# Low-key product of the banded and differential logits: 64 or 128 rows

## Chip, cores and metric

The kernel runs on one core of a Trainium2 chip. The metric is the device time of one execution in microseconds (us), as the median of several runs. The engines go by the profile's names: PE is TensorE's matmuls and PEld its weight loads, DVE is VectorE, ACT is ScalarE, POOL is GpSimd, SP is SyncE, which issues the loads of weights.

## What is computed

The program is a bidirectional encoder of two layers over 512 tokens with 1024 features, in float32. In each layer come a feed-forward block, three attentions whose gated outputs are added, a second feed-forward block and an embedding gate. The change touches two of the attentions. Cut to their logits (the first is banded, a token sees those at most 128 away):

```python
# windowed grouped-query attention: 16 heads of 64 columns, 4 heads of keys
logits = jnp.einsum('bqkgd,bskd->bkgqs', qj, kj).astype(jnp.float32) * scale + bias
logits = jnp.where(valid, logits, NEG_INF)
...
# differential attention: 8 heads, two maps (c) of 64 columns in each
logits = jnp.einsum('bqhcd,bkhcd->bchqk', qj, k).astype(f32) * scale + bias
probs = jax.nn.softmax(logits, axis=-1)
attn = probs[:, 0] - lam * probs[:, 1]
```

Both contract over 64 columns. The scale is 1/8.

## The kernel before

**Split operands.** PE takes operands in a reduced format (float32r). A float32 operand is therefore split into two parts, hi (a rounded copy, made on ACT) and lo (the rest, a subtraction on DVE), whose sum is the operand. A product then takes three matmuls: hi by hi, lo by hi, hi by lo. All of them go through one helper, `mm`, so that nearly every matmul has line L165 in the profile; they are told apart by the names of their tiles.

**Two parts in one product.** A head of 64 columns fills only half of the 128 rows of the array. `q_pair` (L541) uses this: for a pair of heads it makes two tiles of queries, of which tile 0 has hi on rows 0 to 63 and lo on rows 64 to 127, and tile 1 the other way round. The keys' hi part lies on both halves. So one matmul of 128 rows computes q_hi k_hi + q_lo k_hi. The second product, q_hi k_lo, takes only the half of the rows on which q_hi lies (`own`): 64 rows. Both add into one bank of PSUM.

**Who makes the low keys.** `swa_k` (L554) makes the windowed keys, 2 heads at a time, and writes k_lo on both halves, with two subtractions for each head. `diff_k` (L590) makes the differential keys of a pair of maps: four copies on ACT (hi of each map on both halves) and two subtractions on DVE (L599), one for each map, each on the map's own half of one tile `kl`.

**Stages.** The names in the profile give layer, kind and head: m0C3s is the bank of logits (s) of differential head 3 in layer 0; A are heads of the latent attention (16), C differential ones (8), B windowed ones (16); p is a head's tile of probabilities, t its transposes (pth and ptl their hi and lo parts), o its output. Each layer's attention runs A, then C, then B. A differential head has 4 blocks of 128 queries and two maps, so 8 logit tiles of 128 x 512. A windowed head has 4 blocks, each with the two or three blocks of keys around it: 128 x 256 at the two ends and 128 x 384 in the middle.

A logit tile goes from PE to DVE (bias added and the row's minimum, L805 or L747), to ACT (exponential and sum, L807 or L749), to POOL and DVE (division by the sum), back to PE (transposes, L635), to ACT and DVE (their hi and lo parts, L638 and L639), and to PE for the values.

**What sets the order.** Other work of PE (projections of queries, keys, values, gates, and the output product) is cut into pieces that a queue, `Filler`, hands out between the steps of the heads; each piece has a due head, and the queue runs at the lowest even pace that meets these. A pair of differential queries and its keys are due one head ahead of their own. After that a scheduler orders each engine's instructions by their dependences. PSUM has five banks for the heads' steps and three for the filling work. Weights come as 456 chunks of 512 KB by SP, split into hi on ACT (L75) and lo on DVE or, in the attention, on POOL (L76). Tiles of 128 x 512 come from 79 slots.

Of the kernel before, what the change touches and what calls it, by code (L numbers as in the profile page):

```python
# [23 lines left out]
T = 512  # L24
TB = T // P
# [11 lines left out]
# columns of the table of small per-partition values, for each layer  # L37
# [8 lines left out]
class Weights:  # L46
    """All weights as one stream of [128, 1024] chunks, in the order of their use: loaded ahead, then split
    into two float32r parts whose sum is the float32 weight."""
# [41 lines left out]
class Filler:  # L90
    """Pieces of tensor-engine work in a queue, run between the steps of the attention: at the least even pace at
    which each piece ends before the step that it is due at."""
# [44 lines left out]
def encoder_kernel(ctx: ExitStack, tc: tile.TileContext, ins, out):  # L137
# [18 lines left out]
    def PS(name, kind=None):  # L156
        """A bank of PSUM: of those of the attention's steps (s), of those of the work between them (a), or of both
        by turns."""
        if kind is None:
            kind = CYCLE[turn[0] % len(CYCLE)]  # L160
            turn[0] += 1
        return psp.tile([P, 512], F32, tag="ps" + kind, name=name, bufs=BANKS[kind])
# [9 lines left out]
    def split(src, name):  # L172
        """src as two float32r tiles."""
        hi, lo = S(name + "h", F32R), S(name + "l", F32R)
        nc.scalar.copy(hi, src)
        nc.vector.tensor_sub(lo, src, hi.bitcast(F32))
        return hi, lo

# [32 lines left out]
    def constants():  # L211
        nc.gpsimd.dma_start(perm, ins["perm"])
        for l in range(L):
            s = slice(l * NH, (l + 1) * NH)
            nc.vector.tensor_scalar(neg_sink[:, s], small[:, l * S_N + S_SINK:l * S_N + S_SINK + NH], -1.0, None, op0=ALU.mult)
            nc.vector.tensor_scalar(sub_gain[:, l:l + 1], col(l, S_SUB), 1.0 - lambda_init(l), None, op0=ALU.mult)
            lv = S(f"lamv{l}")
            nc.gpsimd.dma_start(lv[:, 0:256], ins["lam"][l])
            e = tiny(f"lam{l}")
            for j in range(2):  # L220
                pr = S(f"lamp{l}{j}")
                nc.vector.tensor_mul(pr[:, 0:64], lv[:, j * 128:j * 128 + 64], lv[:, j * 128 + 64:j * 128 + 128])
                nc.vector.tensor_reduce(e[:, j:j + 1], pr[:, 0:64], axis=AX.X, op=ALU.add)
            nc.scalar.activation(e[:, 2:4], e[:, 0:2], AF.Exp)
            # -(exp(a) - exp(b) + init)
            nc.vector.tensor_scalar(e[:, 4:5], e[:, 3:4], -lambda_init(l), None, op0=ALU.add)
            nc.vector.tensor_sub(neg_lam[:, l:l + 1], e[:, 4:5], e[:, 2:3])
# [10 lines left out]
    def bias_vectors():  # L238
        """The bias of each head over the distance, negated; in the window's, 1e30 outside it."""
        for i in range(3):  # L240
            ps = PS(f"bv{i}")
            heads = slice(0, NH) if i == 0 else slice(NH, NH + NHD)
            n = heads.stop - heads.start
            nc.tensor.matmul(ps[0:n, :], tab[0][0:33, heads], oh[i][0:33, :], start=True, stop=True)
            bv = S(f"bvs{i}")
            nc.vector.tensor_copy(bv[0:n, :], ps[0:n, :])  # L246
            if i == 0:
                nc.gpsimd.dma_start(bias_s, bv[0:n, :])  # L248
            else:
                nc.gpsimd.dma_start(bias_d[:, (i - 1) * 512:i * 512], bv[0:n, :])  # L250
        for vec, copies in ((bias_s, copies_s), (bias_d, copies_d)):
            for i in range(vec.shape[0]):
                nc.gpsimd.dma_start(copies[i], vec[i:i + 1, :].to_broadcast([P, vec.shape[1]]))

    def strip(vec, row, cols, tag, bufs, name):
        """[128, cols]: the head's vector at 127 - p + c, from the copies of it that lie one after the other."""
        t = sb.tile([P, cols], F32, tag=tag, name=name, bufs=bufs)
        n = vec.shape[2]
        at = vec[row, 0:1, 127:128]
        nc.gpsimd.dma_start(t, bass.AP(tensor=at.tensor, offset=at.offset, ap=[[n - 1, P], [1, cols]]))  # L260
        return t

# [1 line left out]
    def root_table():  # L264
        """Loads the square root's table ahead of its use."""
        tc.keep_in_program_order(nc.scalar.activation(tiny("root")[:, 0:1], eps, AF.Sqrt))
# [7 lines left out]
    class Norm:  # L274
        """Root mean square over the features (partitions and tiles), for all tokens."""
# [13 lines left out]
        def add_last(self, src, c):  # L289
            """The columns c of the last tile."""  # L290
            sq = S(f"{self.name}sq{self.i}{c.start}")
            nc.scalar.activation(sq[:, c], src[:, c], AF.Square)
            self.engine.tensor_tensor(self.acc[:, c], self.acc[:, c], sq[:, c], op=ALU.add)
# [18 lines left out]
    class Prep:  # L312
        """The tiles of h as they end: gained and split; the norm's factor comes in after the product."""
# [18 lines left out]
    def proj(ps, w, z, i0=0, n=KT, cols=P):  # L332
        """ps += (128 columns of weights)^T z over n k tiles; yields the work done."""
        wh, wl = w
        for k in range(n):
            c = slice(i0 + k * cols, i0 + k * cols + cols)
            mm3(ps, wh[:, c], wl[:, c], z[k][0], z[k][1], k == 0, k == n - 1)
            if side:
                side.popleft()()
            yield 3  # L340

    def together(pss, ws, z):
        """Several such products, a k tile of each at a time."""
        gens = [proj(ps, w, z, cols=ps.shape[0]) for ps, w in zip(pss, ws)]
        for _ in range(KT):
            for g in gens:
                next(g)
# [59 lines left out]
    def mix(l, prep, p2):  # L407
# [3 lines left out]
        # per-layer input: 0.5 * p W, kept in DRAM until the layer's end  # L411
# [34 lines left out]
        # latents  # L446
# [32 lines left out]
        # keys of a pair of heads, three pairs by turns: rows 0-63 | 64-127 are (own, rope) or (rope, own)  # L479
# [23 lines left out]
        # pieces of work for the tensor engine  # L503
        merged = [None] * KT

        def mla_v(g):
            wh, wl = W.get(("mla_v", l, g))
            vs = [S(f"{name}va{g}_{tb}", F32R) for tb in range(TB)]
            for tb in range(TB):
# [7 lines left out]
                # a pair of heads: hi lo | lo hi  # L517
# [25 lines left out]
        def q_pair(key, at, j):  # L543
            """Two 64-wide queries, times -1/8: (hi, lo) and (lo, hi) on the two halves of the rows."""
# [22 lines left out]
        def swa_v():  # L567
            ws = W.get(("vb", l, 0), ("vb", l, 1))
            for tb in range(TB):
# [10 lines left out]
                for j in range(2):  # L580
                    # a head: hi lo hi
# [8 lines left out]
        def diff_k(j):  # L590
# [3 lines left out]
            kl = S(f"{name}kc{j}l", F32R)  # L594
            for e in range(2):
                own = halves[e]
                for r in halves:
                    nc.scalar.copy(ks[e][r], ps[own])  # L598
                nc.vector.tensor_sub(kl[own], ps[own], ks[e][own].bitcast(F32))  # L599
# [25 lines left out]
        class Head:  # L625
# [22 lines left out]
            def out64(self, i, lhs, gated):  # L648
                """Values of 64 columns as (hi, lo) or (lo, hi): the two halves of the rows are added. Both heads of
                a pair end on the rows that they have in the merged output."""  # L650
# [64 lines left out]
        class Swa(Head):  # L715
# [16 lines left out]
            def logits(self):  # L732
# [3 lines left out]
                own = halves[i % 2]  # L736
                m, sums = tiny(f"{self.name}m"), tiny(f"{self.name}s")
                self.p = []
                for q in range(TB):
# [5 lines left out]
                    mm(ps, qs[own, c], kl[own, k0:k1], False, True)  # L745
# [34 lines left out]
        class Diff(Head):  # L780
# [10 lines left out]
            def logits(self):  # L791
# [4 lines left out]
                for q in range(TB):  # L796
                    c = slice(q * P, (q + 1) * P)
                    bs = self.strip[:, (TB - 1 - q) * P:(TB - 1 - q) * P + T]
                    for e in range(2):
                        own, x = halves[e], e * TB + q  # L800
                        ps = PS(f"{self.name}s{q}{e}", "s")
                        mm(ps, qs[e][:, c], ks[e], True, False)
                        mm(ps, qs[e][own, c], kl[own], False, True)
# [47 lines left out]
        # the heads' steps, and what has to be there before them  # L851
# [12 lines left out]
        for due, key, units, gen in sorted(work, key=lambda x: x[0]):  # L864
            # a pair's keys overwrite those of three pairs before
# [10 lines left out]
        for n, hd in enumerate(heads + [None]):  # L876
# [6 lines left out]
            def run_steps(upto):  # L883
                """What is left of the head before, once so many quarters of this one's logits are under way."""
                while steps and STEP_AT[steps[0][0]] <= upto:
                    steps.pop(0)[1]()
# [31 lines left out]
    def w_out(l):  # L918
        """Four output tiles at a time, over the merged tiles in their order; two of these in each piece."""
# [27 lines left out]
    def ple(l, prep, after, last=None):  # L947
# [6 lines left out]
        for d in range(KT):  # L954
# [8 lines left out]
            if d == KT - 1 and last is not None:  # L963
                # the columns in two halves, for a short way to the end
# [24 lines left out]
    for l in range(L):  # L989
# [24 lines left out]
        def last(d, c):  # L1014
            if c.stop == T:
                # the table of the square root is loaded by the time of the norm
# [25 lines left out]
# latent norms: k tiles of other products between their squares and their sums  # L1042
LEAD = 16
# logit tiles after which the finished ones are normalised
NORMALISE = {"Mla": 2, "Swa": 4, "Diff": 4}
# the shares of a head's filling work that go between its logits and after its transposes
# [5 lines left out]
def _chunk(ins, key):  # L1052
    """A weight chunk of the stream: [128, up to 1024], rows of the weight on the partitions."""
# [85 lines left out]
def build(nc, L):  # L1139
    """The program; the arrays' shapes; the order of the weight chunks."""  # L1140
# [39 lines left out]
```

## Time and profile before

| | before |
|---|---|
| median of 3 runs | 3098.61 us (3098.36 to 3099.18) |
| span of the profiled execution | 3096.5 us, 2.1 us under that median |
| granted clock of TensorE, mean | 0.998 |
| PE, PEld, DVE busy | 3056.6, 2463.9, 1812.5 us |
| ACT, POOL busy | 1423.1, 748.1 us |
| layer 0: A heads / C heads / B heads | 444 to 712 / 712 to 924 / 924 to 1110 us |
| layer 1: C heads / B heads | 2245 to 2456 / 2456 to 2643 us |

The page is of one execution; the trace has no time of its own for that execution besides the span, which runs from the first instruction to the last. The bounds of the stages are read from the starts of the heads' first logits and, at the end, of the last head's values; neighbouring stages overlap by some microseconds, since the steps of one head end in the next one.

### The profile page before, as it was taken

The numbers are of one execution on the slowest core, as the hardware profiler recorded it, in microseconds if no ns is written. First come the engines' busy times: TensorE is split into PE (matmuls) and PEld (weight loads), VectorE is DVE, ScalarE is ACT, GpSimd is POOL, SyncE is SP. The second block draws the span as 40 slices with busy tenths as digits, with TensorE's granted clock in tenths as the row PEclk, the third lists the DMA queues.
The fourth block names the chain that finished last, engine by engine and source line by source line (L and its number), as shares of the span: only waits on it lengthen the run. The fifth ranks groups of instructions, "written<-read, shape, count | busy, mean of one in ns | idle before, by whom it ended". The sixth has DMA issues, their size and how long they took to land.

```text
span 3096.5 us, 37450 instructions
## 1 busy us (share of the span) xinstructions
PE 3056.6 (99%) x14206; PEld 2463.9 (80%) x14206; DVE 1812.5 (59%) x2812; ACT 1423.1 (46%) x2511; POOL 748.1 (24%) x709
## 2 busy tenths in 40 slices
PE   8999999999999999999999999999999999999997
PEld 7888878887777788888888887788877777888886
DVE  6444586535686665444664445765467766654446
ACT  4322356645666653223432223565556666422234
POOL 0010014444445440000200001244444445200003
PEclk9999999999999999999999999999999999999999
DMA  4263431112122233333333334211222122333332
GB/s 151 97 222 99 136 109 59 58 62 80 61 74 80 66 105 96 97 101 95 123 102 96 96 96 152 89 55 55 75 73 72 61 66 66 116 95 96 99 99 89
DMA packets 81524, 287.74 MB, mean 93 GB/s; under 512 B 10382, under 2 KB 12430, under 8 KB 81344
## 3 DMA queue, kind: packets, MB, share of 16 engines
q1 hardware_dynamic: 66960, 240.42, 24.7%
q0 software_dynamic: 12080, 42.00, 3.9%
q10 hardware_dynamic: 2304, 2.94, 0.3%
q8 instruction: 111, 1.82, 0.2%
q14 instruction: 69, 0.57, 0.1%
HBM read 274.76 MB, written 18.94 MB: 95 GB/s over the span
## 4 chain that ended last, share of the span: by engine, by line
PE 95%; DVE 2%; ACT 2%; issue 1%; POOL 0%; DMA 0%; ACTq 0%; DVEq 0%; POOLq 0%
PE ffn10g L165 4%; PE ffn10u L165 4%; PE ffn21g L165 4%; PE ffn20g L165 4%; PE ffn21u L165 4%; PE ffn20u L165 4%; PE ffn21d L165 4%; PE ffn11d L165 4%; PE ffn20d L165 4%; PE ffn10d L165 4%; PE ffn11u L165 4%; PE ffn11g L165 4%; PE wo L165 3%; PE ple L165 3%; PE m1qc L165 2%; PE m0qc L165 2%
## 5 line engine op out<-in xcount | busy, mean ns | idle before, releaser
L75 ACT CAST whi<-wraw 128x1024 fp32r<-128x1024 f32 x456 | 478.2, 1051 | 1093.8 <-issue 379.7
L76 DVE TENSOR_TENSOR wlo<-wraw,whi 128x1024 fp32r<-128x1024 f32 x312 | 383.6, 1232 | 124.2 <-ACT whi L75 123.8
L76 POOL TENSOR_TENSOR wlo<-wraw,whi 128x1024 fp32r<-128x1024 f32 x144 | 351.2, 2441 | 411.2 <-ACT whi L75 375.9
L287 POOL TENSOR_TENSOR pg1sq<-pg1sq,pg1sq 128x512 f32<-128x512 f32 x7 | 11.1, 1586 | 345.0 <-ACT pg1sq L282 345.0
L287 POOL TENSOR_TENSOR pg0sq<-pg0sq,pg0sq 128x512 f32<-128x512 f32 x7 | 11.1, 1586 | 345.0 <-ACT pg0sq L282 345.0
L419 POOL DMA_DIRECT2D h_dram<-wo0h x8 | 4.3, 541 | 341.2 <-DVE wo0h L371 341.2
L371 DVE SCALAR_TENSOR_TENSOR x<-ffn10d,x 128x512 f32<-128x512 f32 x48 | 32.9, 690 | 40.9 <-PE ffn10d L165 40.9
L371 DVE SCALAR_TENSOR_TENSOR wo0h<-ffn11d,wo0h 128x512 f32<-128x512 f32 x48 | 32.9, 690 | 40.9 <-PE ffn11d L165 40.9
L371 DVE SCALAR_TENSOR_TENSOR wo1h<-ffn21d,wo1h 128x512 f32<-128x512 f32 x48 | 32.9, 690 | 38.7 <-PE ffn21d L165 38.7
L371 DVE SCALAR_TENSOR_TENSOR wo0h<-ffn20d,wo0h 128x512 f32<-128x512 f32 x48 | 32.9, 690 | 38.1 <-PE ffn20d L165 38.0
L388 DVE TENSOR_TENSOR ffn20u<-ffn20u,f_0r 128x512 f32<-128x512 f32 x22 | 15.2, 691 | 62.0 <-PE ffn20u L165 62.0
L388 DVE TENSOR_TENSOR ffn21u<-ffn21u,f_1r 128x512 f32<-128x512 f32 x22 | 15.2, 691 | 62.0 <-PE ffn21u L165 62.0
L419 POOL DMA_DIRECT2D h_dram<-x x8 | 4.3, 540 | 190.3 <-DVE x L371 190.3
L388 DVE TENSOR_TENSOR ffn10u<-ffn10u,f_0r 128x512 f32<-128x512 f32 x22 | 15.2, 691 | 59.8 <-PE ffn10u L165 59.8
L388 DVE TENSOR_TENSOR ffn11u<-ffn11u,f_1r 128x512 f32<-128x512 f32 x22 | 15.2, 691 | 59.5 <-PE ffn11u L165 59.5
L386 DVE TENSOR_TENSOR ffn20g<-ffn20g,f_0r 128x512 f32<-128x512 f32 x22 | 15.2, 692 | 47.0 <-PE ffn20g L165 46.9
L386 DVE TENSOR_TENSOR ffn21g<-ffn21g,f_1r 128x512 f32<-128x512 f32 x22 | 15.2, 692 | 46.6 <-PE ffn21g L165 46.6
L386 DVE TENSOR_TENSOR ffn10g<-ffn10g,f_0r 128x512 f32<-128x512 f32 x22 | 15.2, 691 | 44.4 <-PE ffn10g L165 44.4
L386 DVE TENSOR_TENSOR ffn11g<-ffn11g,f_1r 128x512 f32<-128x512 f32 x22 | 15.2, 690 | 44.5 <-PE ffn11g L165 44.5
L287 POOL TENSOR_TENSOR f_1sq<-f_1sq,f_1sq 128x512 f32<-128x512 f32 x14 | 21.0, 1501 | 58.5 <-ACT f_1sq L282 58.3
L248 POOL DMA_DIRECT2D bias_s<-bvs x1 | 0.5, 519 | 142.5 <-DVE bvs L246 142.5
L598 ACT CAST m0kc<-m0kc 64x512 fp32r<-64x512 f32 x32 | 18.5, 580 | 17.2 <-PE m0kc L165 7.9
(5072 smaller groups left out, 10401.3 us busy)
## 6 DMA issues: line engine op xcount, KB each, us to landing
wraw<-in_wall SPq DMA_DIRECT2D x456, 512.0 KB, 3.5
copies_s<-bias_s POOLq DMA_DIRECT2D x16, 256.0 KB, 7.5
copies_d<-bias_d POOLq DMA_DIRECT2D x8, 512.0 KB, 12.8
h_dram<-x POOLq DMA_DIRECT2D x8, 256.0 KB, 2.9
pp_dram<-m0ppt POOLq DMA_DIRECT2D x8, 256.0 KB, 5.6
wo0h<-h_dram POOLq DMA_DIRECT2D x8, 256.0 KB, 4.8
ple0p<-pp_dram POOLq DMA_DIRECT2D x8, 256.0 KB, 4.6
h_dram<-wo0h POOLq DMA_DIRECT2D x8, 256.0 KB, 2.7
```

The source lines that it names most:

```text
L75: self.nc.scalar.copy(hi, raw)
L76: self.lo_engine.tensor_tensor(lo, raw, hi.bitcast(F32), op=ALU.subtract)
L165: nc.tensor.matmul(ps, lhsT, rhs, start=start, stop=stop, skip_group_check=True)
L248: nc.gpsimd.dma_start(bias_s, bv[0:n, :])
L287: self.engine.tensor_tensor(self.acc, self.acc, sq, op=ALU.add)
L371: nc.vector.scalar_tensor_tensor(h[d], ps, 0.5, h[d], op0=ALU.mult, op1=ALU.add)
L386: nc.vector.tensor_mul(g1, pg, rb)
L388: nc.vector.tensor_mul(u1, pu, rb)
L419: nc.gpsimd.dma_start(h_dram[d], h[d])
L598: nc.scalar.copy(ks[e][r], ps[own])
```

## The change

The second product now takes all 128 rows, with k_lo on both halves: it computes q_hi k_lo + q_lo k_lo, so the small product of the two low parts comes in as well. The windowed keys are as before. `diff_k` now makes two tiles of low keys for each pair, one for each map, with the map's k_lo on both halves. This takes four subtractions for each pair where there were two, and one slot more. The rest of the diff takes out comments.

```diff
             ks = [S(f"{name}kc{j}{e}", F32R) for e in range(2)]
-            kl = S(f"{name}kc{j}l", F32R)
+            kl = [S(f"{name}kc{j}l{e}", F32R) for e in range(2)]
             for e in range(2):
                 own = halves[e]
                 for r in halves:
                     nc.scalar.copy(ks[e][r], ps[own])
-                nc.vector.tensor_sub(kl[own], ps[own], ks[e][own].bitcast(F32))
+                for r in halves:
+                    nc.vector.tensor_sub(kl[e][r], ps[own], ks[e][own].bitcast(F32))
             got["kc", j] = (ks, kl)
...
                 ks, kl = got["kb", i // 4]
-                own = halves[i % 2]
...
                     mm(ps, qs[:, c], ks[:, k0:k1], True, False)
-                    mm(ps, qs[own, c], kl[own, k0:k1], False, True)
+                    mm(ps, qs[:, c], kl[:, k0:k1], False, True)
...
                     for e in range(2):
-                        own, x = halves[e], e * TB + q
+                        x = e * TB + q
                         ps = PS(f"{self.name}s{q}{e}", "s")
                         mm(ps, qs[e][:, c], ks[e], True, False)
-                        mm(ps, qs[e][own, c], kl[own], False, True)
+                        mm(ps, qs[e][:, c], kl[e], False, True)
```

The instructions of PE stay the same in number, those of DVE change at `diff_k`, and the scheduler then places some rows otherwise. SP and POOL keep their order, and so do PE and DVE in the windowed heads. On DVE, at the first pair of differential keys of layer 0, behind the reductions of latent head A11 and ahead of the transposes' lo parts of head A10, there stood:

```order
L691 TENSOR_REDUCE m0A11m_4851<-m0A11s3_4896 128x1
L697 RECIPROCAL m0A11s_4852<-m0A11s_4852 128x2
L599 TENSOR_TENSOR m0kc0l_4908<-m0kc0_4825,m0kc00_4906 64x512
L599 TENSOR_TENSOR m0kc0l_4908<-m0kc0_4825,m0kc01_4907 64x512
L639 TENSOR_TENSOR m0A10ptl0_4934<-m0A10t0_4928,m0A10pth0_4933 128x512
L639 TENSOR_TENSOR m0A10ptl1_4943<-m0A10t1_4937,m0A10pth1_4942 128x512
```

In the changed program the same place on DVE reads (lines from there on are one higher; m0kc0l0 and m0kc0l1 are the two tiles of low keys):

```order
L692 TENSOR_REDUCE m0A11m_4851<-m0A11s3_4896 128x1
L698 RECIPROCAL m0A11s_4852<-m0A11s_4852 128x2
L600 TENSOR_TENSOR m0kc0l0_4908<-m0kc0_4825,m0kc00_4906 64x512 x2
L600 TENSOR_TENSOR m0kc0l1_4909<-m0kc0_4825,m0kc01_4907 64x512 x2
L640 TENSOR_TENSOR m0A10ptl0_4937<-m0A10t0_4931,m0A10pth0_4936 128x512
L640 TENSOR_TENSOR m0A10ptl1_4946<-m0A10t1_4940,m0A10pth1_4945 128x512
```

Each row of low keys has become two, at the same place between the same neighbours. On PE, in the logits of differential head C1, whose tiles alternate with the filling product m0gc (a gate), there stood:

```order
L165 MATMUL m0C1s11_6153<-m0kc1l_5282,m0qc11_5225 128x512
L165 MATMUL m0gc4_6107<-m0u4h_2767,whi112_5973 128x512
L165 MATMUL m0gc4_6107<-m0u4h_2767,wlo112_5974 128x512
L165 MATMUL m0gc4_6107<-m0u4l_2768,whi112_5973 128x512
L165 MATMUL m0C1s20_6168<-m0kc10_5280,m0qc10_5224 128x512
L165 MATMUL m0C1s20_6168<-m0kc1l_5282,m0qc10_5224 128x512
L165 MATMUL m0gc4_6107<-m0u5h_2774,whi112_5973 128x512
L165 MATMUL m0gc4_6107<-m0u5h_2774,wlo112_5974 128x512
L165 MATMUL m0gc4_6107<-m0u5l_2775,whi112_5973 128x512
L165 MATMUL m0C1s21_6177<-m0kc11_5281,m0qc11_5225 128x512
```

And the same stretch of PE in the changed program:

```order
L165 MATMUL m0C1s11_6168<-m0kc1l1_5286,m0qc11_5228 128x512
L165 MATMUL m0gc4_6122<-m0u4h_2767,whi112_5985 128x512
L165 MATMUL m0gc4_6122<-m0u4h_2767,wlo112_5986 128x512
L165 MATMUL m0gc4_6122<-m0u4l_2768,whi112_5985 128x512
L165 MATMUL m0gc4_6122<-m0u5h_2774,whi112_5985 128x512
L165 MATMUL m0gc4_6122<-m0u5h_2774,wlo112_5986 128x512
L165 MATMUL m0gc4_6122<-m0u5l_2775,whi112_5985 128x512
L165 MATMUL m0C1s20_6183<-m0kc10_5283,m0qc10_5227 128x512
L165 MATMUL m0C1s20_6183<-m0kc1l0_5285,m0qc10_5227 128x512
L165 MATMUL m0gc4_6122<-m0u6h_2781,whi112_5985 128x512
```

The logit tile m0C1s20 has gone behind the next three rows of the gate. The order gives the output's shape alone, so the second product reads the same in both; how many rows of the array it takes doesn't show here.

## The prediction

> **What bounds the kernel now.** I read the page first: which engine is busy, and whose work makes up the chain that ended last.
>
> ```profile
> PE 3056.6 (99%) x14206; PEld 2463.9 (80%) x14206; DVE 1812.5 (59%) x2812; ACT 1423.1 (46%) x2511; POOL 748.1 (24%) x709
> PE 95%; DVE 2%; ACT 2%; issue 1%; POOL 0%; DMA 0%; ACTq 0%; DVEq 0%; POOLq 0%
> ```
>
> TensorE (PE) is busy for 3056.6 of 3096.5 us and carries 95% of the chain. So time comes off the kernel where PE's own instructions get shorter. The average says little about the two stages that the change touches, so I read next the busy time in stretches: the differential heads and the windowed heads, of layer 0 and then of layer 1 (columns: stretch, its length, then PE, weight loads, VectorE (DVE), ScalarE (ACT), GpSimd (POOL)).
>
> ```profile
> core 0: us, PE busy (x) PEld busy (x) DVE busy (x) ACT busy (x) POOL busy (x), PEclk, DMA share, GB/s
> 712.00:924.00 212.00, 210.80 (x1003) 155.57 (x1002) 151.95 (x279) 134.51 (x260) 92.95 (x73) 1.00 0.23 71
> 924.00:1110.00 186.00, 184.59 (x883) 140.07 (x882) 119.70 (x293) 123.06 (x302) 92.51 (x103) 1.00 0.22 68
> 2245.00:2456.00 211.00, 209.79 (x998) 154.72 (x997) 153.50 (x278) 133.72 (x258) 91.49 (x71) 1.00 0.21 67
> 2456.00:2643.00 187.00, 185.60 (x887) 140.59 (x886) 120.18 (x295) 122.81 (x302) 92.81 (x103) 1.00 0.21 67
> ```
>
> PE is busy all through there at a granted clock of 1.00, and no other engine passes 73%. The list of waits for PE over both stages of layer 0 is short:
>
> ```profile
> PE m0C4o L165 <- DVE m0C4ptl L639: 1.2, 1, 1.2
> PE m0B5o L165 <- DVE m0B5ptl L639: 0.7, 1, 0.7
> PE m0B6o L165 <- DVE m0B6ptl L639: 0.5, 1, 0.5
> ```
>
> PE waits for others 2.4 us of 398. But a busy PE isn't PE at its peak, since the ends of matmuls are modelled: the start of one to the start of the next tells what each really takes. So the last view is PE's order of time, around two logit tiles. First a differential head (columns: start in us, duration, then line, operation, tiles, rows*columns of the stationary operand, moving operand):
>
> ```profile
> 711.76 0.39 PE L165 MATMUL m0gc<-m0u1l,whi 128*128 128x512 f32 x1
> 711.99 0.39 PE L165 MATMUL m0gc<-m0u2h,whi 128*128 128x512 f32 x1
> 712.21 0.39 PE L165 MATMUL m0gc<-m0u2h,wlo 128*128 128x512 f32 x1
> 712.44 0.39 PE L165 MATMUL m0gc<-m0u2l,whi 128*128 128x512 f32 x1
> 712.67 0.39 PE L165 MATMUL m0C0s<-m0kc,m0qc 128*128 128x512 f32 x1
> 712.99 0.50 PE L165 MATMUL m0C0s<-m0kc0l,m0qc 64*128 64x512 f32 x1
> 713.41 0.50 PE L165 MATMUL m0gc<-m0u3h,whi 128*128 128x512 f32 x1
> 713.75 0.39 PE L165 MATMUL m0gc<-m0u3h,wlo 128*128 128x512 f32 x1
> 713.97 0.39 PE L165 MATMUL m0gc<-m0u3l,whi 128*128 128x512 f32 x1
> ```
>
> A 128-row product of 512 columns takes (712.67 - 711.76) / 4 = 0.228 us from start to start. Where the 64-row product stands, three steps are long: 0.32 us before it, 0.42 us for itself, 0.34 us behind it. From 712.67 to 713.75 that is 1.08 us, where three steps of 0.228 would make 0.68: **0.40 us lost around one 64-row product.** The same in a windowed head, with 256 and 384 columns:
>
> ```profile
> 945.79 0.28 PE L165 MATMUL m0B1s<-m0kb00h,m0qb 128*128 128x256 f32 x1
> 945.99 0.38 PE L165 MATMUL m0B1s<-m0kb00l,m0qb 64*128 64x256 f32 x1
> 946.30 0.50 PE L165 MATMUL m0gb<-m0u0h,whi 128*128 128x512 f32 x1
> 946.64 0.40 PE L165 MATMUL m0gb<-m0u0h,wlo 128*128 128x512 f32 x1
> 946.87 0.39 PE L165 MATMUL m0gb<-m0u0l,whi 128*128 128x512 f32 x1
> 947.10 0.34 PE L165 MATMUL m0B1s<-m0kb00h,m0qb 128*128 128x384 f32 x1
> 947.37 0.43 PE L165 MATMUL m0B1s<-m0kb00l,m0qb 64*128 64x384 f32 x1
> 947.74 0.51 PE L165 MATMUL m0gb<-m0u1h,whi 128*128 128x512 f32 x1
> 948.08 0.40 PE L165 MATMUL m0gb<-m0u1h,wlo 128*128 128x512 f32 x1
> ```
>
> What these sizes take with no 64-row product beside them, the values of head B0 show:
>
> ```profile
> 960.78 0.34 PE L165 MATMUL m0B0o<-m0B0ptl,m0vb 128*128 128x384 f32 x1
> 960.96 0.35 PE L165 MATMUL m0B0o<-m0B0pth,m0vb 128*128 128x384 f32 x1
> 961.14 0.34 PE L165 MATMUL m0B0o<-m0B0ptl,m0vb 128*128 128x384 f32 x1
> 961.32 0.28 PE L165 MATMUL m0B0o<-m0B0pth,m0vb 128*128 128x256 f32 x1
> 961.44 0.28 PE L165 MATMUL m0B2s<-m0kb00h,m0qb 128*128 128x256 f32 x1
> 961.56 0.28 PE L165 MATMUL m0B0o<-m0B0ptl,m0vb 128*128 128x256 f32 x1
> ```
>
> 384 columns take 0.18 us from start to start, 256 columns 0.12 us. So for 256 columns the three steps take 946.64 - 945.79 = 0.85 us for 0.12 + 0.12 + 0.228 = 0.47, a loss of 0.38; for 384 columns 948.08 - 947.10 = 0.98 us for 0.18 + 0.18 + 0.228 = 0.59, a loss of 0.39. The loss hardly depends on the columns: it belongs to going into the 64-row form and out of it. The Trainium skill, TensorEngine Tiling (Array Packing), section Key Properties, has a name for it: a change of tiling mode drains TensorE. It gives no length, and the sum doesn't use it.
>
> **The change part by part.** How many such products there are, and what the low keys cost on DVE:
>
> ```profile
> L165 PE MATMUL m0C0s<-m0kc0l,m0qc x8: 492/498/500, 713.0 to 723.1; 64*128 64x512 f32 x8
> L165 PE MATMUL m0B0s<-m0kb00l,m0qb x4: 380/410/442, 924.4 to 931.4; 64*128 64x256 f32 x2, 64*128 64x384 f32 x2
> L599 DVE TENSOR_TENSOR m0kc0l<-m0kc,m0kc x2: 685/690/694, 612.7 to 614.6; 64x512 fp32r<-64x512 f32 x2
> L599 DVE TENSOR_TENSOR m1kc7l<-m1kc,m1kc x2: 673/684/694, 2404.7 to 2406.7; 64x512 fp32r<-64x512 f32 x2
> ```
>
> *Second products at 128 rows.* A differential head has 8, and there are 8 heads in 2 layers: 128 products, 128 x 0.40 = 51.2 us. A windowed head has 4 (2 of each size), and there are 16 heads in 2 layers: 64 x 0.38 + 64 x 0.39 = 49.3 us. No transition is left, so I count the whole loss as gone: 100.5 us, on PE, which sets the end. The 128-row second product was never run in this place; its nearest rows are the values of B0 above, which also put hi and lo parts into one bank with a new stationary operand each time, at the plain step. Bounds: if I misread the steps by 0.01 us each way, 256 x 0.41 = 105 us; at the other end nothing goes (first rival).
>
> *Operands.* The queries of both stages already hold hi on one half and lo on the other, and the windowed keys' low part already lies on both halves; nothing is added there. In the differential stage each pair of keys gets 2 more subtractions on DVE: 2 x 8 x 2 layers = 32 at 0.69 us = 22 us, half of it in each layer. DVE has room: 152.0 + 11.0 = 163 us of a stage of 212 us, or of 212 - 25.6 = 186.4 us when the losses are gone (87%). I cost them at nothing: low keys are made about a head or more ahead (those of C0 at 612.7, their first use at 713.0). Behind them on DVE are queued, for C0, the four subtractions of head A10's transposes, which A10's values wait for; PE has differential values to compute meanwhile. If that cover fails each time, 16 pairs x 1.38 us = 22 us come back. The bank that holds the raw keys is released 1.4 us later; of the three banks of the filling work no wait by PE is in the list above, so again zero, within the same 22 us.
>
> *Slots and queues.* One more slot for each pair of keys, of 79 that are handed out; SP's and POOL's orders are unchanged, so no load moves past another. I take zero.
>
> *What is late next.* PE's 398 us for each layer's two stages become about 348, and the others have the same work in less time: DVE 163 of 186.4 and 119.7 of 161, ACT 134.5 of 186.4 and 123.1 of 161. DVE keeps 23 us idle in the differential stage instead of 60, so some of its results will come late. PE's waits of 2.4 us for each layer I take to rise by 3 us: a choice between no rise and the case in which DVE must keep half of its 60 us of idle time, where the stage takes 163 + 30 = 193 us, 6.6 us over its 186.4, 13 us for both layers. For the windowed heads half of ACT's idle time (31 us) gives 154 us, under 161: nothing.
>
> **Sum.** The profiled execution spans 3096.5 us, 2.1 us under the median of 3098.6, so I carry the difference over: 3098.6 - 100.5 + 6 = **3004 us**.
>
> **The rivals.**
> *Rows cost nothing, so nothing changes (0.05).* If the 0.40 us belongs to the second product as such (its new stationary operand, the same bank), it stays: 3098.6 us, or a few more for DVE. For it: the long steps are seen only at these products. Against it: B0's values change operand and share a bank too, at 0.18 and 0.12 us. The Trainium skill, TensorE: Matmul & The Clock Gate, section Why this matters for your kernels, says that a K=32 product takes the time of one with K=128; by that rule alone the change gives 3098.6 us. The row here disagrees: 0.42 us against 0.228.
>
> *DVE's chain sets the pace (0.04), the side of slower.* Place: the differential heads, from logits over DVE's reduction, ACT's exponentials and the transposes to the values. If that chain sets the stage's length and PE's long steps only fill it, their end turns into waits, in the windowed heads too, and the 32 subtractions lengthen the chain: 3098.6 + 22 = 3121 us. It decides if DVE has no idle time that can be given up, that is if the stage can't get under 212 us with 163 us of DVE work. Against it: 2.4 us of PE waits in 398.
>
> *The same, in the differential stage alone (0.06).* Its 51 us go to waits, the windowed stage's 49.3 us arrive: 3098.6 - 49.3 = 3049 us. For it: DVE comes to 87% there. Against it: even at 87% it has slack, and the logits tiles have filling work between them.
>
> *Two halves at once (0.01).* If a 64-row product left half of the array to its neighbour, 128 rows would cost half a step each: 128 x 0.114 + 64 x 0.09 + 64 x 0.06 = 24 us, 3123 us. The trace has no such overlap: starts lie 0.42 us apart. The Trainium skill, TensorEngine Tiling (Array Packing), section When to Use Tiling, recommends two tiles of rows for a contraction of 64, which speaks against this change; it needs two such products side by side, and here each stands alone between 128-row ones.
>
> **How the numbers follow.** The forecast has 0.84. Its range: below, 3098.6 - 105 = 2994, and 2 us for waits that go as well: 2992. Above, 100.5 us saved, 13 us for DVE's idle time and 22 us for late low keys: 3098.6 - 100.5 + 35 = 3033; I close at 3034. The other cases hold 0.16 and stay outside. A change of 0.2% (6 us) is about what a measurement can tell here. Faster: 0.84 + 0.06 = 0.90; the same: 0.05; slower: 0.04 + 0.01 = 0.05.
>
> **What would show it.** In PE's order of time, the second logits product must stand as 128*128, the steps around it at 0.23 us (512), 0.18 (384) and 0.12 (256); the differential stage near 187 us and the windowed near 161; the low keys' line with 4 subtractions of 0.69 us for each pair; PE's waits in those stages under 10 us for each layer. Long steps at a 128*128 product would make the first rival right; short steps with new PE waits for DVE in their place, the second or third. An A stage or a feed-forward that moved would be something that I haven't seen.

## The result and the profile after

| | before | after |
|---|---|---|
| median | 3098.89 us (4 runs) | 3021.6 us (3021.23 to 3022.21, 4 runs) |
| ratio to before | | 0.9752, 95% interval 0.9738 to 0.9765 |
| span of the profiled execution | 3096.5 us | 3019.7 us |
| differential heads, layer 0 / 1 | 211.5 / 211.6 us | 193.7 / 195.3 us |
| windowed heads, layer 0 / 1 | 186.5 / 186.9 us | 164.3 / 164.8 us |

The change takes 77.3 us off; the forecast was 3004 us, a gain of 94.5. The stages here are cut at the start of the heads' first logits and of the last head's last value product. By them the differential heads gained 17.7 and 16.3 us, the windowed ones 22.3 and 22.1 us, and the latent heads ahead of them lost 1.0 us in each layer: 76.4 us in all, and the spans differ by 76.8.

First the steps. This is PE's order of time in the kernel after, at the first logit tile of differential head C0 and at one of windowed head B1 (start in us, duration, line, operation, tiles, rows*columns of the stationary operand):

```profile
713.54 0.39 PE L165 MATMUL m0gc<-m0u2l,whi 128*128 128x512 f32 x1
713.77 0.39 PE L165 MATMUL m0C0s<-m0kc,m0qc 128*128 128x512 f32 x1
714.00 0.39 PE L165 MATMUL m0C0s<-m0kc0l,m0qc 128*128 128x512 f32 x1
714.22 0.39 PE L165 MATMUL m0gc<-m0u3h,whi 128*128 128x512 f32 x1
714.45 0.39 PE L165 MATMUL m0gc<-m0u3h,wlo 128*128 128x512 f32 x1
...
930.85 0.28 PE L165 MATMUL m0B1s<-m0kb00h,m0qb 128*128 128x256 f32 x1
930.97 0.28 PE L165 MATMUL m0B1s<-m0kb00l,m0qb 128*128 128x256 f32 x1
931.09 0.40 PE L165 MATMUL m0gb<-m0u3h,whi 128*128 128x512 f32 x1
931.33 0.40 PE L165 MATMUL m0gb<-m0u3h,wlo 128*128 128x512 f32 x1
```

The second product stands as 128*128, and no step around it is long: 713.77 to 714.45 is 0.68 us for three steps where there were 1.08, and 930.85 to 931.33 is 0.48 where there were 0.85. The loss of 0.38 to 0.40 us at each second product is gone.

Then what came in its place. The stretches of the two stages (length, then PE, weight loads, DVE, ACT, POOL), and the waits of PE in both stages of layer 0, which were 2.4 us before:

```profile
713.80:907.50 193.70, 186.90 (x1001) 158.51 (x999) 158.67 (x288) 132.39 (x261) 92.90 (x73) 1.00 0.26 78
907.50:1072.00 164.50, 162.53 (x888) 137.30 (x887) 120.22 (x293) 122.19 (x302) 93.80 (x104) 1.00 0.25 76
```

```profile
PE m0C7s L165 <- DVE m0C7m L805: 1.6, 1, 1.6
PE m0C3s L165 <- DVE m0C3m L805: 1.4, 2, 0.8
PE m0C7s L165 <- DVE m0C5og L838: 1.3, 1, 1.3
PE m0C3o L165 <- DVE m0C3ptl L640: 0.9, 1, 0.9
PE m0C6o L165 <- DVE m0C6ptl L640: 0.8, 1, 0.8
PE m0B5o L165 <- DVE m0B5ptl L640: 0.7, 1, 0.7
PE m0vc L165 <- DVE m0kc6l L600: 0.6, 1, 0.6
PE m0B4o L165 <- ACT m0B4pth L639: 0.6, 1, 0.6
PE m0B6o L165 <- DVE m0B6ptl L640: 0.5, 1, 0.5
PE m0C1s L165 <- DVE m0C1m L805: 0.2, 1, 0.2
```

They are 8.6 us now, 6.2 us more; in layer 1 they went from 2.4 to 9.8 us, 7.4 us more. Nearly all are for DVE. DVE is busy for 158.7 of 193.7 us in the differential stage (82%). The low keys' line shows the added work, four subtractions for each pair at the duration that they had:

```profile
L600 DVE TENSOR_TENSOR m0kc0l<-m0kc,m0kc x4: 683/688/695, 612.8 to 616.2; 64x512 fp32r<-64x512 f32 x4
```

### The profile page after: what moved, and what is told of

Its sections match the earlier page's. It is cut to its first block, busy times and chain, and to the rows that moved or that the text cites. A ratio compares the mean times of both kernels' runs of the same rounds, so it can differ in the third digit from the quotient of the medians.

```text
span 3019.7 us, 37502 instructions
## 1 busy us (share of the span) xinstructions
PE 2966.6 (98%) x14206; PEld 2463.6 (82%) x14206; DVE 1837.0 (61%) x2844; ACT 1418.5 (47%) x2511; POOL 749.0 (25%) x709
## 4 chain that ended last, share of the span: by engine, by line
PE 88%; DVE 6%; ACT 4%; issue 2%; POOL 0%; DMA 0%; ACTq 0%; DVEq 0%; POOLq 0%
PE ffn10g L165 4%; PE ffn10u L165 4%; PE ffn21g L165 4%; PE ffn20g L165 4%; PE ffn21u L165 4%; PE ffn20u L165 4%; PE ffn21d L165 4%; PE ffn11d L165 4%; PE ffn10d L165 4%; PE ffn20d L165 4%; PE ffn11g L165 4%; PE ffn11u L165 4%; PE wo L165 3%; PE ple L165 3%; PE m1ga L165 1%
```

## The experiments

After the result the theory was: each visit to the 64-row form costs PE 0.40 us; all of that went, and some 24 us (100.5 less 76.4) came back as waits for DVE, most of it through the 22 us of added subtractions. The rivals: the loss belongs to each second product, however it is placed; and the waits come from PE's shorter steps against the same chain over DVE and ACT, whatever the low keys cost.

**The stages apart.** The differential heads alone:

```diff
-                    mm(ps, qs[:, c], kl[:, k0:k1], False, True)
+                    own = halves[i % 2]
+                    mm(ps, qs[own, c], kl[own, k0:k1], False, True)
```

> The change in the differential heads alone: low keys on both halves with 4 subtractions, 128 rows there, 64 rows still in the windowed heads. Theory (each visit to the 64-row form costs 0.40 us, part of it is given back to waits for VectorE): the differential stage shortens as in the full change, by 17.7 us in each layer, and the stage ahead of it loses its 1.1 us: 3098.9 - 2 x 16.6 = 3066 us, give or take 4. Rival (the two stages' gains depend on each other, since freed time moves work between them): outside 3058 to 3074.

Measured: 3066.89 us (ratio 0.9897, interval 0.9883 to 0.9912), in the theory's range.

The windowed heads alone, with `diff_k` as before:

```diff
-                        mm(ps, qs[e][:, c], kl[e], False, True)
+                        own = halves[e]
+                        mm(ps, qs[e][own, c], kl[own], False, True)
```

> The change in the windowed heads alone: 128 rows there, 64 rows and 2 subtractions still in the differential heads. It adds no work to any engine. Theory: 2 x 22.3 us as in the full change, 3098.9 - 44.6 = 3054 us, up to the whole 49.3 us (3050). If rows cost nothing: 3099.

Measured: 3054.47 us (ratio 0.9856, interval 0.9842 to 0.9871), as the theory had it. The two gains against 3098.46 us, which is the kernel before as run beside these two, are 31.6 and 44.0 us. They add up to 75.6, within 2 us of the full change, so the stages don't depend on each other beyond that. In the windowed heads, where no work is added anywhere, 44 of 49.3 us arrive; in the differential ones 31.6 of 51.2.

**The added subtractions.** Alone, with both second products at 64 rows:

```diff
-                        mm(ps, qs[e][:, c], kl[e], False, True)
+                        own = halves[e]
+                        mm(ps, qs[e][own, c], kl[e][own], False, True)
...
-                    mm(ps, qs[:, c], kl[:, k0:k1], False, True)
+                    own = halves[i % 2]
+                    mm(ps, qs[own, c], kl[own, k0:k1], False, True)
```

> The added subtractions alone: low keys on both halves with 4 subtractions for each pair, but both second products still take 64 rows. Theory (hidden while PE has its long steps, so the added work costs only where VectorE is near its limit): 3099 to 3104 us. Rival (VectorE's chain sets the pace of the differential stage): 3098.9 + 22 = 3121 us.

Measured: 3098.34 us, ratio 0.9998 (0.9989 to 1.0008). The rival, by which DVE's chain sets the pace of that stage (3121 us), falls: while PE has its long steps, 11 us more of DVE's work in each layer don't lengthen the kernel. But the zero is a sum of two parts. From the start of the latent heads' logits to that of the differential heads', layer 0 takes 269.6 us here where it took 268.6, with two new waits for DVE of 0.6 us in all. The differential heads take 210.4 us where they took 211.5, because the wait of 1.2 us at C4's values is gone in the new order, which is luck. The latent heads lose this 1.0 us in the full change and in the run with the differential heads alone too, which have the four subtractions, and not in the run with the windowed heads alone, which has two.

And taken away under the full change: one tile of low keys for a pair, each map's part on its own half.

```diff
-            kl = [S(f"{name}kc{j}l{e}", F32R) for e in range(2)]
+            kl = S(f"{name}kc{j}l", F32R)
...
-                for r in halves:
-                    nc.vector.tensor_sub(kl[e][r], ps[own], ks[e][own].bitcast(F32))
+                nc.vector.tensor_sub(kl[own], ps[own], ks[e][own].bitcast(F32))
...
-                        mm(ps, qs[e][:, c], kl[e], False, True)
+                        mm(ps, qs[e][:, c], kl, False, True)
```

> 128 rows in both stages, but the differential low keys as before the change: one tile for a pair, each map's low part on its own half, 2 subtractions. The second product then multiplies the queries' low half by the other map's low keys, which differs from the full change in the product of the two low parts alone. Theory (of the 24 us that came short of the 100.5, most are the added 22 us of VectorE work, which has no cover where VectorE is at 85%): 3021.6 - 12 to 18 = 3004 to 3010 us. Rival (the missing part comes from PE being shorter against the same chain over VectorE and ScalarE, whatever the low keys cost): 3018 to 3022 us.

Measured: 3018.24 us (ratio 0.9741, 0.9725 to 0.9757). The theory asked for 3004 to 3010. It falls on the rival's side (3018 to 3022), so the subtractions are not what most of the missing 24 us went to; that part of the theory falls. For their price, both kernels were run once more on one chip:

> The full change again, beside the next kernel on the same chip, for the price of the 32 added subtractions: 3021.6 us.

> 128 rows in both stages with shared low keys and 2 subtractions for each pair, again. Theory as it now stands (the subtractions cost 3 us of the 24 that came short): 3 to 4 us under the run before it, 3018.2 us. Rival (the difference lay in the chips): within 1 us of it.

Measured: 3022.01 us (3021.19 to 3023.91) and 3018.22 us (3017.53 to 3019.02). The subtractions cost 3.8 us. Of these, 2.0 us are in the latent heads, which take 268.6 and 268.7 us again with shared keys, and 1.5 us in the differential heads, which take 192.9 and 194.6 us. The version with shared low keys is the fastest of all that ran. It keeps the 128 rows without any added work, at the price that its smallest term is a wrong one: the queries' low part meets the other map's low keys.

Its waits in the differential stage of layer 0 come to 6.3 us in the list, where the full change has 6.8; these are the four at logits:

```profile
PE m0C7s L165 <- DVE m0C7m L804: 1.6, 1, 1.6
PE m0C7s L165 <- DVE m0C5og L837: 1.3, 1, 1.3
PE m0C3s L165 <- DVE m0C3m L804: 1.0, 2, 0.5
PE m0C6s L165 <- DVE m0C6m L804: 0.9, 1, 0.9
```

**What a visit costs.** The kernel before, with the 64-row products of the two maps side by side:

```diff
-                        own, x = halves[e], e * TB + q
-                        ps = PS(f"{self.name}s{q}{e}", "s")
-                        mm(ps, qs[e][:, c], ks[e], True, False)
-                        mm(ps, qs[e][own, c], kl[own], False, True)
+                        x = e * TB + q
+                        if e == 0:
+                            both = [PS(f"{self.name}s{q}{y}", "s") for y in range(2)]
+                            for y in range(2):
+                                mm(both[y], qs[y][:, c], ks[y], True, False)
+                            for y in range(2):
+                                mm(both[y], qs[y][halves[y], c], kl[halves[y]], False, True)
+                        ps = both[e]
```

> The kernel before, with 64 rows everywhere, but in the differential heads the two maps' first products stand together and their two 64-row products behind them, so that 128 visits to the 64-row form become 64. Theory (the 0.40 us is paid for going in and out of the form, once for each visit): 64 x 0.40 = 26 us less, 3098.5 - 26 = 3073 us. Rival (each 64-row product pays it, wherever it stands): 3098 us. A third case: the two products lie on different halves of the rows and run at the same time, then another 64 x 0.23 = 15 us go: 3058 us.

Measured: 3073.91 us (ratio 0.9919, 0.9904 to 0.9933), the theory's number to a microsecond. But its steps say otherwise. PE's order of time there (x2 are two matmuls in one row; the last line is the tile's own row over the same visit, with the starts of its two products):

```profile
713.87 0.61 PE L165 MATMUL m0C0s<-m0kc,m0qc 128*128 128x512 f32 x2
714.42 0.50 PE L165 MATMUL m0C0s<-m0kc0l,m0qc 64*128 64x512 f32 x2
714.85 0.50 PE L165 MATMUL m0gc<-m0u3h,whi 128*128 128x512 f32 x1
715.18 0.39 PE L165 MATMUL m0gc<-m0u3h,wlo 128*128 128x512 f32 x1
```

```profile
L165 PE MATMUL m0C0s<-m0kc0l,m0qc x2: 492/495/498, 714.4 to 714.4; 64*128 64x512 f32 x2
```

Both 64-row products start at 714.4 and together are over in the 0.50 us that one takes: they lie on different halves of the rows and run at the same time. From 713.87 to 715.18 the visit takes 1.31 us. Four plain steps of 0.228, with the two 64-row products counted as one, make 0.91, so the visit loses the same 0.40 us as one with a single product. Against five plain steps (1.14) it loses 0.17 us, where two visits lost 0.80. With 64 such visits that would be 40 us, the third case on record; only 25.1 arrive (3099.01 less 3073.91). In each layer 3 of the 32 pairs came apart in the scheduler's order, which is some 4 us of it, and PE's waits in this stage rose here too, in layer 0 from 1.2 to 5.0 us; the rest, some 4 us, has no row. So the total met the theory's number by chance, while the steps show the third case: the loss belongs to the visit and not to each product, which lets the first rival fall, and two half-height products side by side do share the array. The Trainium skill, TensorEngine Tiling (Array Packing), section When to Use Tiling, recommends exactly that for a contraction of 64, and the trace agrees where the two stand together. A single one between 128-row products has nothing to share with.

**Where the rest went.** In the kernel after, PE waits 1.61 us at 894.6 for a bank of head C7's logits. DVE's order of time there:

```profile
890.11 0.69 DVE L805 CUSTOM_DVE_ANT_0 m0C7p<-m0C7s,m0C7b 128x512 f32<-128x512 f32 x1
890.72 0.09 DVE L805 DVE_READ_ACCUMULATOR2_ANT m0C7m<- 128x1 f32 x1
890.74 3.35 DVE L846 RECIPROCAL m0C4r<-m0C4r 128x512 f32<-128x512 f32 x1
894.12 0.68 DVE L551 SCALAR_TENSOR_TENSOR m0qb<-m0qb,m0qb 64x512 fp32r<-64x512 f32 x1
894.84 0.75 DVE L847 SCALAR_TENSOR_TENSOR m0C4r<-m0C4og,sub_gain,m0C4r 128x512 f32<-128x512 f32 x1
895.50 0.68 DVE L805 CUSTOM_DVE_ANT_0 m0C7p<-m0C7s,m0C7b 128x512 f32<-128x512 f32 x1
```

Between two reductions of C7's logits (L805), each of which lets a bank go, stands the norm of head C4 with a reciprocal of 3.35 us. The reduction that frees the bank starts at 895.50, and PE goes on at 896.25. That gave a second theory: the reciprocal keeps DVE from freeing banks in time. Its test moves the root and the reciprocal to ACT:

```diff
-                    nc.scalar.activation(r, ss, AF.Sqrt, bias=eps, scale=1.0 / P)
-                    nc.vector.reciprocal(r, r)
+                    nc.scalar.activation(r, ss, AF.Ln, bias=eps, scale=1.0 / P)
+                    nc.scalar.activation(r, r, AF.Exp, scale=-0.5)
```

> 128 rows in both stages and shared low keys (3018.2 us), and the root of the differential heads' norm taken by ScalarE as exp(-0.5 ln x) in two passes, in place of ScalarE's root and VectorE's reciprocal of 3.35 us; the number of table loads is the same. Theory (the reciprocal is what keeps VectorE from freeing logit banks in time): PE's waits for VectorE at logit tiles in the differential stage go, some 5 us in each layer: 3006 to 3010 us. Rival (VectorE is late in general, or the chain is): 3015 to 3019 us.

Measured: 3029.18 us (ratio 0.9774, 0.9759 to 0.9788), 11 us slower than with the reciprocal and outside both cases on record. DVE has 12 us less to do in the stage (141.2 us busy between 713 and 912 us, where the run with the reciprocal has 153.1 between 712 and 905), the logits' waits at C3 and C6 are gone, and others stand elsewhere:

```profile
PE m0C3t L635 <- DVE m0C4m L804: 3.2, 2, 1.8
PE m0C4o L165 <- DVE m0C4ptl L639: 2.1, 1, 2.1
PE m0C7s L165 <- DVE m0C7m L804: 1.6, 1, 1.6
```

But the run doesn't take away what the theory names. This is DVE's order of time at C7 in it:

```profile
890.37 0.69 DVE L804 CUSTOM_DVE_ANT_0 m0C7p<-m0C7s,m0C7b 128x512 f32<-128x512 f32 x1
...
893.72 1.07 DVE L846 SCALAR_TENSOR_TENSOR m0C4r<-m0C4og,sub_gain,m0C4r 128x512 f32<-128x512 f32 x1 [2.65 <-ACT m0C4r L845]
...
896.33 0.69 DVE L804 CUSTOM_DVE_ANT_0 m0C7p<-m0C7s,m0C7b 128x512 f32<-128x512 f32 x1
```

The norm's factor now comes from ACT, and DVE waits 2.65 us for it in the place where the reciprocal took 3.35. The reduction stands behind the norm as before, and PE waits the same 1.6 us. DVE's waits for the factors of C0, C1 and C3 rose too, from 1.9 us each to 2.9, 4.4 and 3.8 us. So the edit made the norm shorter on DVE and later on ACT, and the second theory is neither shown nor refuted by it. What both traces show at C7 is the norm ahead of the reduction in DVE's order.

Two attempts at more cover and more room came out slower. The share of filling work between a head's logits raised:

```diff
-SHARES = {"Mla": (0.3, 0.6), "Swa": (0.5, 0.3), "Diff": (0.3, 0.5)}
+SHARES = {"Mla": (0.3, 0.6), "Swa": (0.5, 0.3), "Diff": (0.5, 0.3)}
```

> 128 rows in both stages and shared low keys (3018.2 us), and a differential head's share of filling work between its logits raised from 0.3 to 0.5, after its transposes lowered from 0.5 to 0.3. Theory (PE waits for banks that VectorE frees late, since the logit tiles now follow each other faster than VectorE's 3.35 us reciprocal lets it read them): more filling work between the tiles takes most of these 5.5 us in each layer: 3006 to 3012 us. Rival (the chain's length sets the stage, and the waits reappear at the transposes and values): 3016 to 3022 us.

Measured: 3048.04 us (3047.28 to 3052.16), outside both cases. The rival has the places right but not the size: most of PE's waits now stand at values and transposes (2.6 us at C4o, 2.4 at C6o, 2.3 at C2o), beside one of 2.8 us at C7's logits. And one bank more for the heads, one less for the filling work:

```diff
-BANKS = {"a": 3, "s": 5}
+BANKS = {"a": 2, "s": 6}
```

> 128 rows in both stages and shared low keys (3018.2 us), with six banks of PSUM for the heads' steps and two for the filling work, instead of five and three. Theory (waits for a bank): each wait for a logit bank shrinks by one tile's time, about 0.7 us: 5 waits in each layer, 3018.2 - 7 = 3011 us, unless the filling work then waits for its two banks, which can cost more than that. Rival (not the banks): 3018 us or more.

Measured: 3057.38 us (3052.94 to 3059.98), on the rival's side; its longest wait in layer 0 is now the filling work's own, 5.2 us in three pieces for the queries' split on DVE. Then the opposite of the raised share, (0.2, 0.6) in the same line:

> 128 rows in both stages and shared low keys (3018.2 us), with a differential head's share of filling work between its logits lowered from 0.3 to 0.2 and after its transposes raised from 0.5 to 0.6: the opposite of the run with 0.5 and 0.3 (3048.0 us). Theory (what PE waits for is set by where the fixed order puts cover; cover moved ahead of the values takes their waits away, but logit tiles then follow each other faster than VectorE frees their banks): waits at the logits rise from 5.0 us in each layer, waits at the values go; 3018 to 3035 us. Rival (the logits' waits come from VectorE's load whatever the cover): under 3018 us.

Measured: 3025.28 us, in the theory's range, but by luck, since the waits went the other way. At the logits they fell, from 4.8 to 2.9 us in layer 0 and from 4.9 to 4.1 in layer 1; at the values they rose, from 0.9 to 2.4 and from 0.8 to 3.5 us. And (0.3, 0.6):

> 128 rows in both stages and shared low keys, with the share between the logits kept at 0.3 and the share after the transposes raised from 0.5 to 0.6. Theory: the logits' waits stay, the values' waits (0.9 us at C6o, in each layer) go: 3014 to 3020 us. Rival (any other order of the same work moves the time by ten us or more, so that no single wait accounts for it): outside 3010 to 3026 us.

Measured: 3033.29 us, outside: the rival's side. The wait at C6's values is gone in layer 0, but not in layer 1 (1.4 us), and the windowed heads, which the theory left out, take 3.4 and 4.2 us longer.

All these do the same work but for the root of the norm, and they lie between 3018 and 3057 us. So what came back is for the most part PE's waits for DVE in an order that the scheduler fixes, and which wait it is changes with every edit. That the time is so sensitive is shown; one instruction as the cause isn't, and whether an order exists that gives the missing 20 us back stays open, since no run kept the order and changed a duration alone.

## Why the prediction was right, point by point

- *What bounds the kernel.* Right: PE's steps set the end, and shortening them shortened the kernel by 77 us.
- *0.40 us around each 64-row product.* Right in place and size: the steps are plain after. The prediction read it at three products; added up over all 256 in the trace before, the steps at them, ahead of them and behind them lose 100.0 us, where it had 100.5. That the loss belongs to the visit to the form, as the prediction put it, is shown by the two products that share one visit: counted as one step, they lose the 0.40 us once.
- *The first rival, rows cost nothing.* It fell with the first rows of the trace. The second product's step went from 0.42 to 0.23 us in the differential head, and in the windowed one, where nothing of the product but its rows changed, from 0.31 to 0.12 us.
- *The 32 subtractions at nothing.* Nearly: 3.8 us under the full change, of the 22 us that the prediction gave as the bound, and no change of the total without it. Over half of it falls in the latent heads, during which the low keys of the first pairs are made. The bank of raw keys, which was costed at zero, is waited for once in each layer (0.6 us, at the low keys of pair 6).
- *What is late next.* The place was right (DVE, the differential heads), the size was not, and this is most of why 77.3 us came and not 94.5. The term was 3 us for each layer; some 12 us came back in each. Of the 25.6 us of the differential heads 7.9 and 9.3 came back in layers 0 and 1, of the 24.65 us of the windowed heads 2.4 and 2.6, and the latent heads lost 1.0 in each, which is the added subtractions'. The listed waits rose by 6.2 and 7.4 us. The list also counts less than a wait costs: for the one of 1.34 us at C7, the product ahead starts at 887.90 and the next at 889.64, which is 1.74 us or 1.51 over a plain step, and the step behind it takes 0.34 instead of 0.23:

```profile
887.90 0.40 PE L165 MATMUL m0C7s<-m0kc7l,m0qc 128*128 128x512 f32 x1
889.64 0.50 PE L165 MATMUL m0C7s<-m0kc,m0qc 128*128 128x512 f32 x1 [1.34 <-DVE m0C5og L838]
889.98 0.40 PE L165 MATMUL m0C7s<-m0kc7l,m0qc 128*128 128x512 f32 x1
```

  That is 0.28 us more than listed for a wait, some 2 us for each layer with eight and nine waits more than before. About 2 us in each layer have no single row. Why the waits came to so much more than the 3 us stays open, as said above; the choice of 3 us rested on DVE's idle share alone.
- *The windowed heads lose nothing.* They kept back 2.4 and 2.6 us of 24.65, though ACT and DVE stay at 73 to 74% there: a share of busy time under a limit doesn't mean that nothing is late.
- *The price of lateness* was worked out from an engine's busy share in the stage. The rows at C7 show a matter of order: DVE, busy for 82% of the stage, has the norm with its 3.35 us reciprocal ahead of the 0.68 us reduction that PE waits for, and is late at that moment.
- *Two halves at once.* Rejected for this change, rightly; but as a mechanism it exists, as the grouped run shows.

## What to carry to other kernels

Read a matmul's cost from start to start, with its neighbours: here a product that used half of the rows cost 0.63 us with what it took from its neighbours, nearly three times a full one of 0.228, because it stood alone between full ones. Either fill the rows, with work that needn't be of use, or put two half-height products on opposite halves side by side. And when the engine that sets the end gets faster, look for a part of the gain (a quarter here) given back to the engines behind it, in places that their busy share doesn't name.

## What the runs showed of the hardware that was not expected

**A lower clock behind a stall of PE.** In the run with the logarithm, PE waited 2.13 us, and the steps behind that were 0.43 us instead of 0.23 for some 3.5 us:

```profile
855.90 0.61 PE L165 MATMUL m0C4o<-m0C4pth,m0vc 128*128 128x512 f32 x2
858.65 0.75 PE L165 MATMUL m0C4o<-m0C4ptl,m0vc 128*128 128x512 f32 x1 [2.13 <-DVE m0C4ptl L639]
...
860.90 0.63 PE L165 MATMUL m0C3ss<-m0C3sql,ones 128*128 128x512 f32 x1
861.33 0.63 PE L165 MATMUL m0gc<-m0u5h,whi 128*128 128x512 f32 x1
861.76 0.58 PE L165 MATMUL m0gc<-m0u5h,wlo 128*128 128x512 f32 x1
862.18 0.39 PE L165 MATMUL m0gc<-m0u5l,whi 128*128 128x512 f32 x1
```

The granted clock (the third number from the end) in the 5 us behind the wait, and after that:

```profile
858.00:863.00 5.00, 4.35 (x12) 3.46 (x13) 3.17 (x5) 3.09 (x5) 0.58 (x1) 0.66 0.34 105
863.00:880.00 17.00, 16.86 (x84) 13.95 (x83) 11.84 (x28) 14.62 (x29) 10.01 (x9) 1.00 0.23 74
```

In the kernel after, the longest wait in these stages is 1.6 us, and their granted clock is 1.00. In the run with the raised share waits of 2.35 us (C2's values) and 2.41 us (C6's) were followed by a clock of 1.00, those of 2.6 and 2.8 us by 0.83 over 10 us. The Trainium skill, TensorE: Matmul & The Clock Gate, section Why this matters for your kernels, warns of gaps over some 3 us; here the clock fell behind 2.13 us once, and didn't behind 2.35 us. So these rows give no fixed length. The profiled executions of the three variants with such waits (logarithm, raised share, six banks) have a mean clock of 0.992 to 0.995, the kernel after 0.998; so a part of their extra time may be clock and not waits. No run held the waits and changed the clock alone.

**DVE instructions stretched.** In the same run, two combinations of probabilities on DVE took 3.95 us, where two took 1.83 us elsewhere in the run, and the low part that PE's 2.13 us wait was for stood behind them:

```profile
854.04 3.95 DVE L816 SCALAR_TENSOR_TENSOR m0C5p<-m0C5p,m0C5r,m0C5p 128x512 f32<-128x512 f32 x2 [0.23 <-POOL m0C5p L623]
857.92 1.27 DVE L639 TENSOR_TENSOR m0C4ptl<-m0C4t,m0C4pth 128x512 fp32r<-128x512 f32 x2
```

POOL was splitting a chunk of weights at that moment (854.65 to 857.45). The kernel before has the same: 9 of its 64 combinations took 2.87 to 2.93 us, and all nine ran beside such a split, while the others took at most 1.18 us. The low parts on DVE (L639) took no more than 0.69 us beside the same splits. That the two get in each other's way is the likely reading; no run took one of them away.
